# A hybrid trunk layer on one core: Hyena convolutions in two lanes that take turns, and the Hyena chunks ahead of queries, keys and values

## The chip, the cores and the metric

The kernel runs on one core of a Trainium2 chip: a matrix engine (PE, with its weight load, PEld), a vector engine (DVE), an activation engine (ACT), a general engine (POOL) and a queue engine (SP) that mostly issues DMAs. The engines run beside one another; each takes its own instructions strictly in the order of its queue. The metric is the time of one execution on the device in microseconds (us), less is better.

## The reference

One layer for 1024 latent tokens and 256 context tokens of width 1024. Half of the mixed width is attention (8 heads of 64), half a Hyena group of 512 channels with two long convolutions in a row, done by FFT:

```python
def _layer(x, mods, attend, norm1_g, w_in, hy_conv_w, hy_conv_b, k_f, filt_bias, ...):
    h = _rmsnorm(x, norm1_g) * (1.0 + sc1) + sh1
    proj = h @ w_in                                   # 1024 -> 3*512 (q, k, v) + 3*512 (hyena)
    hy = _dwconv3(proj[..., 3 * ATTN_WIDTH:], hy_conv_w, hy_conv_b)
    a = attend(q, k, v)
    hyo = _hyena(hy, k_f, filt_bias)
    merged = concat([_rmsnorm(a, ...), _rmsnorm(hyo, ...)])
    x = x + g1 * (merged @ w_out)
    h2 = _rmsnorm(x, norm2_g) * (1.0 + sc2) + sh2
    u = _dwconv3(h2 @ w_up, ffn_conv_w, ffn_conv_b)
    return x + g2 * ((silu(gate) * up) @ w_down)

def _hyena(hy, k_f, filt_bias):
    x1, x2, v = jnp.split(hy, 3, axis=-1)
    z = x1 * _long_conv(v, k_f[:, 0], filt_bias[0])
    return x2 * _long_conv(z, k_f[:, 1], filt_bias[1])
```

Latent tokens attend to an 8 x 16 neighbourhood of a 16 x 64 grid, with a learned relative bias, and to 256 cached context keys in the same softmax. The filters k_f come from a small network and an FFT of their own.

## The kernel before

The program is written once for the whole layer; a scheduler of the language then orders each engine's queue by priorities (the order of the text, which high_priority shifts ahead) and by the tiles' dependencies.

**Projection.** The product with w_in is cut into 24 chunks of 128 output channels; the first is done earlier, 23 stand in this stage. Each chunk loads its weights (tile wr, SP), splits them in two parts (wh on ACT, wl on POOL or DVE) and multiplies them in three passes with the tokens held in hh and hl (lines 116 to 118, 72 matmuls into a PSUM bank psp). A chunk of hyena channels (hy_chunk, lines 650 to 680) also does the width-3 convolution on ACT and DVE, folds the sequence (tile fo), turns it over PE and stores it in DRAM (lxd for latent, cxd for context tokens). A chunk of queries, keys or values (qkv, lines 682 to 719) goes through ACT copies to DRAM (qd, kd, vd). The loop at lines 737 to 756 takes for each j of 0 to 3 in turn one chunk of q, hyena, k, hyena, v, hyena, and after j = 0 the three tables of relative bias (rpb_frames: 16 small loads each and one store, rpw in DRAM). In between, at low density, run the filters' FFTs (psfA, psfB), which keep their data in the pool filt on the right side of the memory, and the products with w_ada.

**Chains.** When the filters are done, their pool is closed and a pool "chain" opens in its place. chain(j), lines 770 to 892, convolves 128 channels twice (o = 0, 1): a forward transform (line 802: 8 matmuls with dftf into a bank pscA, in 4 pieces; ACT makes two twisted copies t, DVE adds them, line 816), a butterfly on DVE (822 to 827), the product with the filter spectrum K loaded from DRAM (836 to 843), a butterfly back (847 to 852) with a twist (857 to 859), and an inverse transform (line 871: 8 matmuls, 2 pieces) with the gate x1 or x2. Each piece holds a bank pscA until ACT and DVE have read it. Chains 0 to 3 are latent, chain 4 (lat false) is all of the context, without the butterflies. Tiles of even and odd chains have different tags (b_ = j % 2), so that two chains may be under way, and each has one tile t (TB = 1). Each chain is written out as a whole, one after another, with a priority of 2000 places ahead. For chains 0 and 1 there are three banks pscA; then these are closed and the chains 2 to 4 have one, because attention takes seven of the eight banks.

**Attention.** Four pairs of heads (attend), each with four blocks of latent queries and the context. A block makes scores (psS, line 1038), adds the bias from a table tb (DVE, line 1059), exponentials (ACT, 1072 and 1073), turns them over PE (psX, 1082), copies them to SBUF (pt: ACT and DVE) and multiplies by values (psav, 999). POOL issues the loads of q, k, vs and of the tables (line 951, 16 per table, three tables per pair).

**Output projection.** Its pool wo_ takes the memory of the pool chain: w_out is loaded (tile wor, SP) and split (wh on ACT, line 1158, wl on DVE, line 1159) after the last chain. Then token sums (psX, line 1187), the products into psd, in two halves (attention's from tile ar, hyena's from tile mr, whose rows y are loaded from hyd, where the chains stored them), norms, then the feed-forward part, which lasts to the end.

Of the kernel before, what the change touches and what calls it, by code (L numbers as in the profile page):

```python
# [11 lines left out]
F32 = mybir.dt.float32  # L12
# [7 lines left out]
P = 128  # L20
# [3 lines left out]
LT = LL + LC  # L24
# [62 lines left out]
def _build(nc, tc, top, V, A, G, T, Q, I, O, dbg, upto):  # L87
# [412 lines left out]
    with ies:  # L500
# [3 lines left out]
        for gi, (s, col, tl) in enumerate(groups):  # L504
            xs = []
            for i in tl:
                src, row, _ = tiles[i]
# [22 lines left out]
            n = P * len(tl)  # L530
# [54 lines left out]
    ip = pool(ies, "ip", reuse_waits="tile")  # L585
# [150 lines left out]

    for j in range(4):
        for which in range(3):
            if j + which > 0:
                qkv(j, which)  # L740
            hy_chunk(which, j)
            if j + which == 0:

                t = ft([P, 512], "tm", bufs=2)
                e = "p a b -> p (a b)"
                Q.dma_start(out=t, in_=I["t_dft"].flatten().rearrange("(p x) -> p x", p=P))
                split(t, dft[0].rearrange(e), dft[1].rearrange(e))
                Q.dma_start(out=dlt, in_=I["t_delta"])
                Q.dma_start(out=nt, in_=I["t_nt"])
                with tc.issue_after(wloads[-1]):  # L750
                    Ws0 = w3load(0)
                filters(hs1, hs2, Ws0)
        cached(j)
        if j == 0:
            for var in range(3):
                rpb_frames(ip.tile([P, LT], F32, tag="fo", name="rp", bufs=1), var)
    fes.close()
    fbk.close()
    cbk = Banks("bkc", "right", "tile", cA=(1, 3))
# [8 lines left out]
    CHP = 2000  # L768

    def chain(j):  # L770

        lat = j < 4
        b_ = j % 2
# [18 lines left out]
        for o in range(2):  # L792
# [3 lines left out]
            for h in range(2):  # L796
                hs = slice(h * P, (h + 1) * P)
                for rp in range(2):
                    pa = bk("cA")
                    xs = slice(rp * 256, (rp + 1) * 256)  # L800
                    for i in range(2):
                        T.matmul(pa[:, i * 256:(i + 1) * 256], dftf[:, i, hs], uv[:, i, xs], start=True, stop=True)
                    pv = pa.rearrange("p (i r c) -> p i r c", i=2, r=2)
                    if not lat:
                        A.copy(Gv[:, h, :, 2 * rp:2 * rp + 2], pv)
                        continue
                    for ri in range(2):
                        r = 2 * rp + ri
                        if r == 0:
                            A.copy(Gv[:, h, :, 0], pv[:, :, 0])  # L810
                            continue
                        c, s, ns = tw_chain(h, r)
                        t = cp.tile([P, 2, P], F32, tag=f"t{b_}", name="t", bufs=TB)
                        A.activation(t[:, 0], pv[:, 1, ri], AF.Copy, scale=ns)
                        A.activation(t[:, 1], pv[:, 0, ri], AF.Copy, scale=s)
                        V.scalar_tensor_tensor(Gv[:, h, :, r], pv[:, :, ri], c, t, op0=ALU.mult, op1=ALU.add)
            if lat:
                ac = s4().rearrange(f4, h=2, i=2, q=2)
                X = s8()
                Xv = X.rearrange(f4, h=2, i=2, q=4)  # L820
                Xf = X.rearrange("p (h x c) -> p h x c", h=2, x=8)
                V.tensor_add(ac, Gv[:, :, :, 0:2], Gv[:, :, :, 2:4])
                V.tensor_sub(Gv[:, :, :, 2:4], Gv[:, :, :, 0:2], Gv[:, :, :, 2:4])
                V.tensor_sub(Xf[:, :, 2:8:5], Gv[:, :, :, 2], Gv[:, :, ::-1, 3])
                V.tensor_add(Xf[:, :, 3:7:3], Gv[:, :, :, 2], Gv[:, :, ::-1, 3])
                V.tensor_add(Xv[:, :, :, 0], ac[:, :, :, 0], ac[:, :, :, 1])
                V.tensor_sub(Xv[:, :, :, 1], ac[:, :, :, 0], ac[:, :, :, 1])
                Y = Gt
            else:
                X = Gt  # L830
                Y = s8()
            Xs = X.rearrange("p (h i x) -> p h i x", h=2, i=2)
            Ys = Y.rearrange("p (h i x) -> p h i x", h=2, i=2)
            for h in range(2):
                Kt = cp.tile([P, 2, 512], F32, tag=f"K{b_}", name="K", bufs=1)
                Q.dma_start(out=Kt.rearrange(f1), in_=(Kd[o, j] if lat else Kc[o])[:, h * 1024:(h + 1) * 1024])
                kr = Kt[:, 0:1].to_broadcast([P, 2, 512])
                ki = Kt[:, 1:2].to_broadcast([P, 2, 512])
                B = s4().rearrange(v2, i=2)
                V.tensor_mul(B, Xs[:, h, ::-1], ki)  # L840
                V.tensor_mul(Ys[:, h], Xs[:, h], kr)
                V.tensor_sub(Ys[:, h, 0], Ys[:, h, 0], B[:, 0])
                V.tensor_add(Ys[:, h, 1], Ys[:, h, 1], B[:, 1])
            if lat:
                ac = s4().rearrange(f4, h=2, i=2, q=2)
                Gf = Gt.rearrange("p (h x c) -> p h x c", h=2, x=8)
                V.tensor_add(ac, Gv[:, :, :, 0:4:2], Gv[:, :, :, 1:4:2])
                V.tensor_sub(Xv[:, :, :, 0:2], Gv[:, :, :, 0:4:2], Gv[:, :, :, 1:4:2])
                V.tensor_add(Gf[:, :, 1:8:6], Xv[:, :, :, 0], Xv[:, :, ::-1, 1])
                V.tensor_sub(Gf[:, :, 3:6:2], Xv[:, :, :, 0], Xv[:, :, ::-1, 1])  # L850
                V.tensor_add(Gv[:, :, :, 0], ac[:, :, :, 0], ac[:, :, :, 1])
                V.tensor_sub(Gv[:, :, :, 2], ac[:, :, :, 0], ac[:, :, :, 1])
                for h in range(2):
                    for r in (1, 2, 3):
                        c, s, ns = tw_chain(h, r)
                        t = cp.tile([P, 2, P], F32, tag=f"t{b_}", name="t", bufs=TB)
                        A.activation(t[:, 0], Gv[:, h, 1, r], AF.Copy, scale=s)
                        A.activation(t[:, 1], Gv[:, h, 0, r], AF.Copy, scale=ns)
                        V.scalar_tensor_tensor(Gv[:, h, :, r], Gv[:, h, :, r], c, t, op0=ALU.mult, op1=ALU.add)  # L859
            if o == 0:  # L860
                x1 = load(1).rearrange(v2, i=2)
                un = s4()
            else:
                x2 = load(2).rearrange(v2, i=2)
                ot = s4().rearrange(v2, i=2)
# [19 lines left out]
            if o == 0:  # L885
                u = un
            elif lat:
                for i in range(2):
                    Q.dma_start(out=hyd[i * 4:i * 4 + 4, :, j * P:(j + 1) * P].rearrange("r p c -> p r c"),
                                in_=ot[:, i].rearrange("p (r c) -> p r c", r=4))  # L890
            else:
                Q.dma_start(out=hyd[8:10].rearrange("i p x -> p i x"), in_=ot)

    for j in range(5):
        if j == 2:
            cbk.close()
            cbk = Banks("bkd", "right", "tile", cA=(1, 1))
        with tc.high_priority(offset=CHP):
            chain(j)
    for _ in ada:  # L900
        pass
    scalevec(A2, n2g, 4)
# [879 lines left out]
```

## Time and profile before

| | us |
|---|---|
| median of 3 timed runs (1921.77 to 1924.47) | 1923.5 |
| the profiled execution | 1925.38 |
| its span (first to last instruction) | 1923.4 |
| PE busy | 1742.3 (91%) |
| weight load busy | 1460.2 (76%) |
| DVE busy | 1358.3 (71%) |
| ACT busy | 893.5 (46%) |
| POOL busy | 371.1 (19%) |

Times in the rows are microseconds from the start of the span. A row of the timeline gives start, duration, engine, line, operation, the tile written and the tiles read, the count, and in brackets how long the engine had stood idle before it and what released it. The granted clock is the share of TensorE's full clock that the chip granted. A float32 matmul of the program shows as two in the trace, one with float32r operands as one. Names are those of the program; s stands for all tiles of the chains (tags s8 and s4).

### The profile page before, as it was taken

How to read it: one execution, taken by the hardware profiler on the slowest of the kernel's cores; microseconds unless marked ns; L12 is line 12 of the kernel's file. 1: busy time of each engine (PE TensorE's matmuls, PEld its weight loads, DVE VectorE, ACT ScalarE, POOL GpSimd, SP SyncE). 2: the span in 40 equal slices, each digit the busy share in tenths (PEclk: the TensorE clock that was granted, in tenths of full speed). 3: DMA queues.
4: the chain of work that ended last, by engine and by line, in shares of the span. 5: the costliest groups of instructions: out<-in, count | busy, mean ns of one | idle time of the engine just before them, and what ended most of it. 6: DMA issues, size and time to landing. Idle time of an engine off the chain costs nothing.

```text
span 1923.4 us, 27377 instructions
## 1 busy us (share of the span) xinstructions
PE 1742.3 (91%) x9999; PEld 1460.2 (76%) x9999; DVE 1358.3 (71%) x2158; ACT 893.5 (46%) x1852; POOL 371.1 (19%) x436
## 2 busy tenths in 40 slices
PE   5899989999993798866799699999999999999997
PEld 1688877888872455443688699999999999788786
DVE  4657637756776877864455888888877777666787
ACT  4654435434342677631445544444444444443352
POOL 2354545541236553200100000000000000000001
PEclk7999989999996999985799799999999999999999
DMA  7424444456445433102622155555322222844663
GB/s 261 137 75 129 130 123 123 133 166 198 132 156 151 107 71 99 48 23 66 208 99 98 55 160 165 165 164 173 113 72 72 72 66 67 295 173 124 200 196 128
DMA packets 207288, 249.75 MB, mean 130 GB/s; under 512 B 26915, under 2 KB 152980, under 8 KB 206898
## 3 DMA queue, kind: packets, MB, share of 16 engines
q1 hardware_dynamic: 196936, 231.86, 37.5%
q0 software_dynamic: 8512, 15.33, 3.2%
q8 instruction: 79, 1.29, 0.3%
q10 hardware_dynamic: 1705, 0.82, 0.2%
q14 instruction: 56, 0.45, 0.1%
HBM read 176.75 MB, written 71.20 MB: 129 GB/s over the span
## 4 chain that ended last, share of the span: by engine, by line
PE 35%; DVE 14%; DMA 8%; issue 4%; ACT 4%; POOL 2%; SPq 0%; DVEq 0%; POOLq 0%; ACTq 0%
PE psd L118 5%; PE psd L116 5%; PE psd L117 5%; DMA wt<-in_w_down_dram 2%; PE psa L116 2%; PE psa L117 2%; PE psa L118 2%; DMA tdr<-wt 2%; POOL tb L951 2%; PE psc L117 1%; PE psc L118 1%; PE psc L116 1%; PE pscA L871 1%; PE psb L117 1%; PE psb L118 1%
## 5 line engine op out<-in xcount | busy, mean ns | idle before, releaser
L116 PE MATMUL psp<-hh,wh 128*128 128x512 f32 (+1 forms) x552 | 202.3, 367 | 2.3 <-ACT wh L121 1.9
L118 PE MATMUL psp<-hh,wl 128*128 128x512 f32 (+1 forms) x552 | 200.0, 363 | 0.9 <-POOL wl L122 0.9
L117 PE MATMUL psp<-hl,wh 128*128 128x512 f32 (+1 forms) x552 | 199.1, 361 | 0.0
L116 PE MATMUL psa<-T,ws 128*128 128x256 f32 (+1 forms) x528 | 166.2, 315 | 3.1 <-ACT rows L1497 3.0
L117 PE MATMUL psa<-T,ws 128*128 128x256 f32 (+1 forms) x528 | 165.8, 314 | 2.8 <-DVE T L1224 2.8
L118 PE MATMUL psa<-T,ws 128*128 128x256 f32 (+1 forms) x528 | 165.2, 313 | 0.0
L1697 POOL TENSOR_TENSOR rs<-rs,mhalf 128x1 f32<-128x1 f32 x10 | 7.7, 772 | 813.9 <-DVE rs L1696 813.9
L116 PE MATMUL psd<-wd,gs 128*128 128x512 f32 x360 | 140.8, 392 | 3.1 <-ACT gs L121 3.1
L117 PE MATMUL psd<-wd,gs 128*128 128x512 f32 x360 | 141.0, 392 | 0.0
L118 PE MATMUL psd<-wd,gs 128*128 128x512 f32 x360 | 123.4, 390 | 2.5 <-DVE gs L122 2.5
L116 PEld LDWEIGHTS psp<-hh,wh 128*128 128x128 f32 x552 | 105.4, 191 | 23.3 <-issue 6.2
L118 PEld LDWEIGHTS psp<-hh,wl 128*128 128x128 f32 x552 | 105.5, 191 | 16.0 <-POOL wl L122 1.2
L116 PE MATMUL psc<-T,ws 128*128 128x384 f32 (+1 forms) x352 | 110.2, 313 | 7.3 <-ACT ws L121 7.3
L117 PEld LDWEIGHTS psp<-hl,wh 128*128 128x128 f32 x552 | 105.6, 191 | 14.2 <-issue 0.4
L117 PE MATMUL psc<-T,ws 128*128 128x384 f32 (+1 forms) x352 | 110.2, 313 | 0.0
L118 PE MATMUL psc<-T,ws 128*128 128x384 f32 (+1 forms) x352 | 110.0, 313 | 0.0
L117 PE MATMUL psb<-T,ws 128*128 128x384 f32 (+1 forms) x352 | 109.9, 312 | 0.0
L118 PE MATMUL psb<-T,ws 128*128 128x384 f32 (+1 forms) x352 | 109.9, 312 | 0.0
L116 PE MATMUL psb<-T,ws 128*128 128x384 f32 (+1 forms) x352 | 109.8, 312 | 0.0
L951 POOL DMA_DIRECT2D tb<-rpw x192 | 100.4, 531 | 35.7 <-DVE m L1059 20.3
L871 PE MATMUL pscA<-s,idft 128*128 128x256 f32 x160 | 55.1, 487 | 56.0 <-DVE s L859 45.1
L116 PEld LDWEIGHTS psa<-T,ws 128*128 128x128 f32 x528 | 101.4, 192 | 4.7 <-ACT rows L1497 4.7
(394 smaller groups left out, 4800.9 us busy)
## 6 DMA issues: line engine op xcount, KB each, us to landing
wada<-in_w_ada_dram SPq DMA_DIRECT2D x48, 512.0 KB
wr<-in_w_up_dram SPq DMA_DIRECT2D x44, 512.0 KB
gr<-gdr SPq DMA_DIRECT2D x44, 320.0 KB
wr<-in_w_in_dram SPq DMA_DIRECT2D x23, 512.0 KB
wt<-in_w_down_dram SPq DMA_DIRECT2D x44, 256.0 KB
tdr<-wt SPq DMA_DIRECT2D x44, 256.0 KB
gdr<-cv SPq DMA_DIRECT2D x22, 512.0 KB
wr<-tdr SPq DMA_DIRECT2D x20, 512.0 KB
```

Of the source, the lines that this page charges most:

```text
L116: T.matmul(out, ah, bh, start=start, stop=False, skip_group_check=True)
L117: T.matmul(out, ah, bl, start=False, stop=False, skip_group_check=True)
L118: T.matmul(out, al, bh, start=False, stop=stop, skip_group_check=True)
L871: T.matmul(pa[:, i * 256:(i + 1) * 256], idft[:, i, h], Ys[:, h, i, xs], start=h == 0, stop=h == 1, skip_group_check=True)
L951: G.dma_start(out=tv[:, :, a * 8:a * 8 + 64], in_=rpw[var, :, 2 * p_:2 * p_ + 2, :, d * 8:d * 8 + 64].rearrange("q h u x -> q (h u) x"))
L1697: G.tensor_tensor(rs, rs, mhalf, op=ALU.pow)
```

## The change

```diff
@@ in the input projection
     for j in range(4):
         for which in range(3):
-            if j + which > 0:
-                qkv(j, which)
             hy_chunk(which, j)
             if j + which == 0:
...
                 filters(hs1, hs2, Ws0)
+    for j in range(4):
+        for which in range(3):
+            if j + which > 0:
+                qkv(j, which)
+            if j == 0:
+                rpb_frames(ip.tile([P, LT], F32, tag="fo", name="rp", bufs=1), which)
         cached(j)
-        if j == 0:
-            for var in range(3):
-                rpb_frames(ip.tile([P, LT], F32, tag="fo", name="rp", bufs=1), var)
@@ in chain(j), four times for each o: behind the forward transform, the filter product,
@@ the butterfly back, and the inverse transform with its stores
+            yield
@@ the loop over the chains
-    for j in range(5):
-        if j == 2:
+            yield
+
+
+    lanes = [(None for j in js for _ in chain(j)) for js in ((0, 2, 4), (1, 3))]
+    turn2 = [0, 0] + [1, 0] * 20 + [0] * 8
+    for n, i in enumerate(turn2):
+        if n == 16:
             cbk.close()
             cbk = Banks("bkd", "right", "tile", cA=(1, 1))
         with tc.high_priority(offset=CHP):
-            chain(j)
+            next(lanes[i], None)
```

All twelve hyena chunks are written first, then the eleven chunks of q, k and v, with a table of relative bias behind each of the first three. chain becomes a generator of eight phases. Lane 0 runs chains 0, 2 and 4, lane 1 chains 1 and 3; after two phases of lane 0 the lanes alternate. The three banks pscA become one after 16 phases: by then chain 0 is written out, chain 1 but for its last phase, and chain 2's first forward transform. In the changed program lines 770 to 890 stand 1 to 5 lines later, and what is behind the chains 9 later (scores at 1047, the transforms at 804 and 876).

The order that the scheduler makes of it, at three places. On PE, behind the last matmul of the projection. The numbers in the names count tiles: before, s_5566 is the first convolution of chain 1, s_5660 and s_5679 its second, s_5800 the first of chain 2.

```order
L871 MATMUL pscA<-s_5566,idft 128x256
L233 MATMUL pstB<-ident,mr_4674 128x128 x2
L671 MATMUL pstB<-ident,fo 128x128 x8
L871 MATMUL pscA<-s_5566,idft 128x256 x3
L677 MATMUL pstB<-ident,fo 128x128 x2
L871 MATMUL pscA<-s_5566,idft 128x256 x3
L802 MATMUL pscA<-s_5660,dftf 128x256 x2
L732 MATMUL pstB<-ident,ck 128x128 x2
L802 MATMUL pscA<-s_5660,dftf 128x256 x6
L871 MATMUL pscA<-s_5679,idft 128x256 x8
L802 MATMUL pscA<-s_5800,dftf 128x256 x2
L1038 MATMUL psS<-k,q 128x264 x2
```

Behind the change, the same place on PE; s_5771 is the first convolution of chain 2, s_5623 the second of chain 1, s_5863 the first of chain 3.

```order
L804 MATMUL pscA<-s_5771,dftf 128x256 x6
L233 MATMUL pstB<-ident,mr_4440 128x128 x2
L704 MATMUL pstB<-ident,qkv 128x128 x2
L804 MATMUL pscA<-s_5771,dftf 128x256 x2
L716 MATMUL pstB<-ident,qkv 128x128 x8
L876 MATMUL pscA<-s_5623,idft 128x256 x4
L732 MATMUL pstB<-ident,ck 128x128 x2
L876 MATMUL pscA<-s_5623,idft 128x256 x4
L1047 MATMUL psS<-k,q 128x264 x2
L1047 MATMUL psS<-k,q 128x288 x2
L804 MATMUL pscA<-s_5863,dftf 128x256 x4
```

Before, a whole second convolution of one chain (forward, then inverse) stands between the projection and the first score; now a forward transform and an inverse one of two different chains do. Ahead of this place PE's queue before has three forward and two inverse transforms, that of the change four and three.

On PE, at the end of attention, before: s_6147 is the second convolution of chain 3, s_6264 to s_6336 both of chain 4, and the rows of line 1187 are the token sums.

```order
L999 MATMUL psav<-pt,vs 64x256 x2
L1187 MATMUL psX<-ones_71,asq 128x2
L1187 MATMUL psX<-ones_71,sq 128x2
L1187 MATMUL psX<-ones_71,asq 128x2
L1187 MATMUL psX<-ones_71,sq 128x2
L871 MATMUL pscA<-s_6147,idft 128x256 x8
L802 MATMUL pscA<-s_6264,dftf 128x256 x8
L871 MATMUL pscA<-s_6283,idft 128x256 x8
L802 MATMUL pscA<-s_6300,dftf 128x256 x8
L871 MATMUL pscA<-s_6336,idft 128x256 x8
```

And with the change, the last chain rows on PE (s_6336 is again the last convolution of chain 4), which stand in the middle of attention:

```order
L1091 MATMUL psX<-ident,Pl_6396 128x128 x2
L876 MATMUL pscA<-s_6336,idft 128x256
L1008 MATMUL psav<-pt,vs 64x256 x2
L1091 MATMUL psX<-ident,Pl_6392 128x128 x2
L1091 MATMUL psX<-ident,Pl_6396 128x128 x2
L1008 MATMUL psav<-pt,vs 64x256 x2
L1091 MATMUL psX<-ident,pc 128x128 x4
L876 MATMUL pscA<-s_6336,idft 128x256 x4
L1008 MATMUL psav<-pt,vs 64x256 x2
```

At this point 108 of the 144 score rows, 242 of the 458 rows into psX and 104 of the 192 into psav have been passed; from here to the token sums PE's queue holds attention only.

On ACT, the split of w_out (tile wh), before, between the last copies of chain 4 and the first of tile ar:

```order
L805 COPY s_6319<-pscA 128x2x256 x4
L881 COPY tt<-pscA 128x256 x2
L1158 ACTIVATE wh_8286<-wor,vec 128x1024
L1158 ACTIVATE wh_8292<-wor,vec 128x1024
L1158 ACTIVATE wh_8298<-wor,vec 128x1024
L1158 ACTIVATE wh_8304<-wor,vec 128x1024
L1251 CAST ar<-at_6387 128x512 x2
```

and with the change, where attention's copies (pt) and exponentials (pcc) stand between and behind its rows:

```order
L1000 COPY pt<-psX 128x512 x3
L1020 COPY lt<-psX 128x128
L1025 COPY bs<-psX 128x512
L1167 ACTIVATE wh_8286<-wor,vec 128x1024
L1000 COPY pt<-psX 128x512 x2
L1167 ACTIVATE wh_8292<-wor,vec 128x1024
L1000 COPY pt<-psX 128x512 x3
L1167 ACTIVATE wh_8298<-wor,vec 128x1024
L1167 ACTIVATE wh_8304<-wor,vec 128x1024
L1000 COPY pt<-psX 128x512
L1112 ACTIVATE pcc,lc<-psS,n 128x256 x4
```

The nine rows of the split moved from behind the chains to the last part of attention.

More of the change, by code (lines that the diff above doesn't have):

```diff
@@ L859, in chain @@
                         V.scalar_tensor_tensor(Gv[:, h, :, r], Gv[:, h, :, r], c, t, op0=ALU.mult, op1=ALU.add)
+            yield
             if o == 0:
@@ L892, in chain @@
                 Q.dma_start(out=hyd[8:10].rearrange("i p x -> p i x"), in_=ot)
-    for j in range(5):
-        if j == 2:
+            yield
+    lanes = [(None for j in js for _ in chain(j)) for js in ((0, 2, 4), (1, 3))]
+    turn2 = [0, 0] + [1, 0] * 20 + [0] * 8
+    for n, i in enumerate(turn2):
+        if n == 16:
             cbk.close()
```

## The prediction

> **What bounds the kernel now.** I read the busy time of each engine by stretches first, then PE's instructions in order of time at the two places where PE stands still, then the stretches of single tiles. The columns of the first view are: stretch, its length, busy time (and instructions) of PE, weight load, DVE, ACT and POOL, the granted clock, DMA share, GB/s.
>
> ```profile
> 570.00:625.00 55.00, 20.99 (x85) 13.56 (x83) 35.55 (x63) 18.67 (x57) 35.87 (x74) 0.72 0.50 141
> 625.00:848.00 223.00, 196.67 (x1256) 115.94 (x1256) 169.35 (x385) 145.59 (x472) 82.22 (x154) 0.99 0.27 71
> 848.00:937.00 89.00, 46.31 (x117) 30.98 (x117) 41.82 (x62) 16.52 (x31) 2.38 (x2) 0.56 0.26 81
> ```
>
> The reader is to see three stretches: the gap between projection and attention, the attention (PE 196.67 of 223 us, 0.88), and a tail of 89 us in which no engine reaches half its time. PE tells what stands there:
>
> ```profile
> 613.30 1.19 PE L871 MATMUL pscA<-s,idft 128*128 128x256 f32 x2 [24.70 <-DVE s L859]
> ...
> 623.42 1.20 PE L1038 MATMUL psS<-k,q 64*128 64x264 f32 x8
> ...
> 847.36 0.36 PE L1187 MATMUL psX<-ones,sq 128*128 128x2 f32 x2
> 860.23 1.22 PE L871 MATMUL pscA<-s,idft 128*128 128x256 f32 x2 [12.51 <-DVE s L859]
> ...
> 923.36 0.63 PE L1187 MATMUL psX<-ones,asq 128*128 128x2 f32 x2 [5.14 <-DVE ria L1190]
> ...
> 936.94 0.80 PE L116 MATMUL psd<-wh,ar 128*128 128x512 f32 x1 [0.77 <-ACT ar L1251]
> ```
>
> In the gap PE holds the scores (L1038) behind chain 1's second convolution and waits 24.70 us for it. In the tail it has nothing but the end of chain 3 and all of chain 4, one step behind another, and the output projection (psd) starts at 936.94. Both are **latencies of one chain at a time**, and both lie on the path.
>
> How much work the chains are shows on the tile that they live in (s; here the columns are PE, weight load, DVE, ACT, clock, DMA share, GB/s), and the last row is one whole context convolution:
>
> ```profile
> 440.00:570.00 130.00, 20.18 (x80) 14.50 (x80) 80.29 (x103) 11.69 (x34) 1.00 0.49 156
> 570.00:625.00 55.00, 17.17 (x52) 11.16 (x52) 31.98 (x50) 8.54 (x25) 0.72 0.50 141
> 625.00:848.00 223.00, 28.24 (x108) 18.71 (x108) 88.97 (x129) 15.51 (x43) 0.99 0.27 71
> 848.00:923.00 75.00, 37.65 (x80) 22.46 (x80) 36.76 (x52) 8.95 (x20) 0.57 0.21 63
> 873.00:896.00 23.00, 15.06 (x32) 8.92 (x32) 10.85 (x15) 2.34 (x4) 0.55 0.30 92
> ```
>
> The DVE column of the first four rows adds up to 238 us, for ten convolutions: 2 x 10.85 for the context, so (238 - 22)/8 = 27 us for each of the eight latent ones. On PE a transform of 16 such matmuls (8 in the program, two passes each) costs 28.24/108 x 16 = 4.2 us in the attention.
>
> **The change part by part.** Nothing is computed more or less. What moves is counted from the order above, and each term is a point in time of the profiled execution.
>
> *End of the projection.* The last projection matmul releases POOL here:
>
> ```profile
> 570.39 0.20 POOL L968 MEMSET Pl<- 128x120 f32 x1 [4.27 <-PE psp L118]
> 572.31 7.37 POOL L951 DMA_DIRECT2D tb<-rpw  x14
> ```
>
> so it ended at 570.4. The order of before has five transforms ahead of that point (three forward, two inverse, less the last matmuls), that of the change seven (four and three). PE is full there (second row below), so two more transforms add 2 x 4.2 = 8.4: **579**. What could shift this is the earlier stall in the first row:
>
> ```profile
> 250.00:300.00 50.00, 40.59 (x207) 32.39 (x207) 26.98 (x44) 23.20 (x53) 27.59 (x20) 0.83 0.41 129
> 440.00:570.00 130.00, 129.03 (x721) 105.27 (x721) 97.72 (x148) 50.64 (x119) 29.07 (x17) 1.00 0.49 156
> ...
> 262.78 10.10 SPq L556 DMA_DIRECT2D rp<-in_rpb_dram  x13
> ...
> 275.03 0.39 SPq L606 DMA_DIRECT2D wr<-in_w_in_dram  x1
> ```
>
> PE loses 9.4 us there, and SP's queue issues 13 bias loads for 10.10 us ahead of the next chunk's weights. The same 48 loads now stand between chunks 16 and 19, ahead of other weight loads: the stall may go (-9), stay, or come twice (+9). I take it as staying. That all hyena chunks run beside the filters puts about 12 x 4 us of convolution on DVE into the first half instead of half of it; PE's cover there is the reason to cost it at nothing, and the +9 holds what it costs if the cover fails.
>
> *First score.* PE's queue now has one forward transform of chain 2 and chain 1's last inverse ahead of the first score, both of which have been prepared by different lanes. DVE's queue, however, has chain work ahead of the first score row: the end of chain 1 and chain 2 up to its filter product, some 25 us of the 27 above. Without any idle that is 25 us; in the gap of before one lane needed 42 us (from 580 to 622) for about as much. Two lanes fill each other's waits, but not all: 33, so **612** instead of 623. The first bias table is ready long before (14 of its 16 loads are issued by 579.7 in POOL's row above, 9 us behind the projection). POOL's queue now has 4 loads of the next pair ahead of the second table, which wait for the first scores; 4 + 16 loads at 0.53 us (7.37/14) are 11 us, and DVE has some 30 us of rows before the second table is read, so they stay hidden.
>
> *Attention with chains.* At the last inverse transform PE's queue of the change has passed 108 of 144 score rows, 242 of 458 rows into psX and 104 of 192 into psav; what follows is attention alone. From the first score to there DVE has 27 x 4 of chains (6 of chain 2's first convolution, then three whole ones and the two of the context: 6 + 81 + 22 = 109 us) and its own work: 169.35 - 88.97 = 80 us in all, of which between 53% and 75% by those counts; scores weigh more on DVE, so 55. Together **165 us**. PE's own work is 196.67 - 28.24 = 168 us, divided like these rows (columns as for s):
>
> ```profile
> 625.00:848.00 223.00, 48.04 (x280) 23.99 (x280) 52.53 (x83) 43.89 (x160) 0.99 0.27 71
> 625.00:848.00 223.00, 78.10 (x484) 53.10 (x484) 21.87 (x32) 45.54 (x88) 0.99 0.27 71
> 625.00:848.00 223.00, 59.23 (x384) 20.79 (x384) 7.15 (x12) 0.99 0.27 71
> ```
>
> (psS, psX, psav). A quarter of the first, 43% of the second (without the 36 rows of the token sums) and 46% of the third remain: 72 of 185, so 66 of the 168. The first part has 102 + 11 transforms x 4.2 = 149 us for PE. DVE has more and is the bound. In the attention of before the busier engine had 0.88 of the time: 165/0.88 = 188, **800**. The bounds: 165 with no idle at all, 217 if DVE stays at the 169.35/223 = 0.76 that it had. What idles it there is the chain's own handshake with ACT, 23.3 us in 24 steps:
>
> ```profile
> L816 DVE SCALAR_TENSOR_TENSOR s<-pscA,tw,t 128x256 f32<-128x256 f32 x24 | 11.5, 481 | 23.3 <-ACT t L815 23.3
> ```
>
> In the new order rows of the other lane or of scores stand between most of these steps, so I go above 0.76.
>
> *Attention alone.* 66/0.88 = 75: **875**. PE reached more where the chains were quiet:
>
> ```profile
> 810.00:847.00 37.00, 35.97 (x227) 22.05 (x228) 22.02 (x38) 20.35 (x59) 0.00 (x0) 0.95 0.01 1
> ```
>
> (0.97, hence 68 as the lower bound). I stay at 0.88 because w_out's split now stands here, nine ACT copies of about 1.1 us and as many DVE rows, and the first waits for a load, 8.39 us in ACT's row of before:
>
> ```profile
> 927.06 2.19 ACT L1158 ACTIVATE wh<-wor,vec 128x1024 fp32r<-128x1024 f32 x2 [8.39 <-DMA wor<-in_w_out_dram]
> ```
>
> With that wait laid open the term is 85 (75 + 8, and 2 for later loads).
>
> *Start of the output projection.* From the first token sum behind the chains to the first psd matmul the rows above show 923.36 to 936.94, 13.6 us at half clock and with the weights still to load. At full clock and with weights ready: 9 (bounds 7 and 14), **884**. What is late next are the hyena rows y, which load only when attention's memory is free; two tokens' attention half of the product (48 matmuls) covers them as before. From psd on nothing changes.
>
> Sum: 936.94 - 884 = 53 us less. The profiled execution took 1925.38 (its span 1923.4), 1.9 over the median of 1923.5; the same 53 from the median give **1871**.
>
> A place where the notes speak against the change. The row first: the 108 matmuls of the chains took 28.24 us at clock 0.99, the 80 of the tail 37.65 at 0.57, 1.8 times as much each. The Trainium skill, TensorE: Matmul & The Clock Gate, section "What's actually happening", says that PE drops to half clock after an idle window of about 3.4 us and needs as long a busy one to return. The trace agrees in the tail. By the rule a first part that DVE bounds, with PE 149/188 busy, could fall to half clock as well; it is a rival below.
>
> **The rivals.**
>
> *DVE stays at 0.76* (217 instead of 188, and the wait for w_out is exposed, +10): 1871 + 39 = 1910. For it: each lane keeps a single t buffer. Against: the interleaved order. 0.14.
>
> *The lanes fill everything*: 25, 165 and 68 in place of 33, 188 and 75: 1871 - 38 = 1833. For it: tens of us in which DVE was full. Against: DVE's queue is in order. 0.10.
>
> *Slower: one PSUM bank for two lanes.* From the change of banks on, both lanes take turns in one bank, through all of the first part. How long it is held shows in chain 2 of before:
>
> ```profile
> 677.55 1.46 PE L871 MATMUL pscA<-s,idft 128*128 128x256 f32 x6
> 680.96 1.99 PE L871 MATMUL pscA<-s,idft 128*128 128x256 f32 x8
> 685.96 1.03 PE L802 MATMUL pscA<-s,dftf 128*128 128x256 f32 x4
> 690.30 1.13 PE L802 MATMUL pscA<-s,dftf 128*128 128x256 f32 x4
> ```
>
> 4.3 us for a forward and 3.4 for an inverse piece; 20 and 12 of them are 127 us, hidden in 188. If DVE's longer queue stretches each hold, the bank decides from 188/127 = 1.5 times on, and the gain is gone at (188 + 53)/127 = 1.9 times; at twice, 254, it is 1871 + 66 = 1937. 0.04.
>
> *Slower: the clock.* All 149 us of PE's first part at the tail's price are 1.8 x 149 = 268 instead of 188: 1951. Break-even is at three quarters of it. Against it:
>
> ```profile
> 640.00:650.00 10.00, 7.20 (x45) 3.70 (x44) 10.00 (x24) 5.39 (x19) 4.99 (x10) 1.00 0.23 39
> ```
>
> PE at 0.72 with DVE full, and the clock is 1.00. 0.03. This is what the rule of the Trainium skill would do here.
>
> *The wait only moves*: attention ends as early, but something else holds psd until about 937, the final time 1923. The rows of the new order between the last score and psd hold no chain and no weight split, so 0.02.
>
> **How the numbers follow.** Forecast 0.67, the rest as given. 0.2% of the time is 3.8 us, about what a measurement of this kernel can tell from no change. Faster by more: 0.67 + 0.14 + 0.10, less 0.01: 0.90; within: 0.03; slower: 0.07. All lower bounds together give 570 + 25 + 165 + 68 + 7 = 835, so 1822; all upper ones 588 + 42 + 217 + 85 + 14 = 946, so 1932; they don't all fall one way. The range takes in the first rival and half of the second: 1840 to 1910.
>
> **What would show it.** The last projection matmul near 579, the first score near 612, no chain row behind the last score, DVE at 0.85 or more and the clock at 1.0 until the last inverse transform near 800, psd from 884 at full clock, and the same 986 us from there to the end. I am wrong if DVE idles on ACT's t as often as before, if attention's copies wait for w_out in ACT's queue, if PE waits for chains before 579, or if the first product of the output projection waits for y.

## The result, and the profile after

The changed kernel takes **1870.95 us** (median of 4 runs, 1868.46 to 1874.61) against 1922.63 us for the one before (4 runs beside them, 1915.45 to 1924.47): ratio 0.9739, 95% interval 0.971 to 0.9769, so 52 us by the medians and 2.6% by the ratio, where 1871 us had been predicted. Its profiled execution took 1868.46 us, with a span of 1866.7.

The total fits to a microsecond, the way there does not. First the stretches of the changed kernel that answer to those of before (stretch, length, busy us of PE, weight load, DVE, ACT and POOL, granted clock, DMA share, GB/s):

```profile
250.00:300.00 50.00, 49.12 (x317) 41.20 (x316) 31.10 (x57) 28.10 (x57) 24.58 (x17) 1.00 0.39 125
567.00:591.00 24.00, 13.91 (x49) 10.78 (x48) 17.23 (x32) 11.67 (x41) 15.62 (x37) 0.72 0.57 151
591.00:793.00 202.00, 159.92 (x865) 95.89 (x863) 167.59 (x348) 112.26 (x362) 96.74 (x181) 0.87 0.41 115
793.00:868.00 75.00, 67.49 (x465) 38.65 (x464) 39.18 (x88) 49.15 (x131) 5.55 (x11) 1.00 0.23 70
868.00:880.00 12.00, 8.87 (x43) 8.64 (x42) 1.25 (x6) 2.78 (x4) 2.38 (x2) 0.62 0.07 24
```

The tail of 89 us with one chain alone is gone: behind the last inverse transform stand 75 us of attention alone, in which PE works 0.90 of the time, and 12 us of token sums. The gap has shrunk from 53 us (570.39 to 623.42) to 24. Row one holds a surprise: PE is nearly full between 250 and 300 us (49.12 of 50 us), where it lost 9.4 us before. Row three holds the other one: the attention with chains takes 202 us, and the clock in it is 0.87.

The points themselves, from the changed kernel's instructions in order of time (start, us, engine, line; in brackets how long the engine stood idle before, and for what):

```profile
567.54 0.20 POOL L977 MEMSET Pl<- 128x120 f32 x1 [9.45 <-PE psp L118]
...
591.53 1.20 PE L1047 MATMUL psS<-k,q 64*128 64x264 f32 x8
...
602.68 2.04 PE L804 MATMUL pscA<-s,dftf 128*128 128x256 f32 x4 [9.95 <-DMA s<-lxd]
...
791.19 1.89 PE L876 MATMUL pscA<-s,idft 128*128 128x256 f32 x8
...
867.92 0.28 PE L1196 MATMUL psX<-ones,asq 128*128 128x2 f32 x2
...
880.73 0.77 PE L116 MATMUL psd<-wh,ar 128*128 128x512 f32 x1
```

| point | before | predicted | measured | the step: predicted, measured |
|---|---|---|---|---|
| last projection matmul | 570.4 | 579 | 567.5 | +8.6, -2.9 |
| first score | 623.4 | 612 | 591.5 | gap 33, 24 |
| end of the last inverse transform | | 800 | 793.1 | attention with chains 188, 201.6 |
| end of attention (first token sum) | 846.7 | 875 | 867.9 | attention alone 75, 74.8 |
| first psd | 936.9 | 884 | 880.7 | 9, 12.8 |
| end of the span | 1923.4 | | 1866.7 | 986.5 before, 986.0 |

Up to psd 56.2 us are saved instead of 53; the errors of the five steps are -11.5, -9, +13.6, -0.2 and +3.8 us and mostly cancel. That the time was met to a microsecond is luck. The experiments ask which of the steps were understood.

### The profile page after: what moved, and what is told of

Same layout as the page of the kernel before. It is cut to its first block, busy times and chain, and to the rows that moved or that the text cites. A ratio compares the mean times of both kernels' runs of the same rounds, so it can differ in the third digit from the quotient of the medians.

```text
span 1866.7 us, 27362 instructions
## 1 busy us (share of the span) xinstructions
PE 1728.6 (93%) x9999; PEld 1453.5 (78%) x9999; DVE 1365.0 (73%) x2158; ACT 891.3 (48%) x1852; POOL 366.3 (20%) x436
## 4 chain that ended last, share of the span: by engine, by line
PE 50%; DVE 22%; DMA 12%; issue 6%; ACT 6%; POOL 2%; SPq 1%; DVEq 0%; ACTq 0%; POOLq 0%
PE psd L116 6%; PE psd L117 6%; PE psd L118 6%; PE psp L116 2%; PE psp L118 2%; PE psp L117 2%; PE psa L116 2%; PE psa L117 2%; PE psa L118 2%; DMA wt<-in_w_down_dram 2%; DMA tdr<-wt 2%; PE psc L117 2%; PE psc L118 2%; PE psc L116 2%; PE psav L1008 1%
## 5 line engine op out<-in xcount | busy, mean ns | idle before, releaser
L116 PE MATMUL psp<-hh,wh 128*128 128x512 f32 (+1 forms) x552 | 201.6, 365 | 1.9 <-ACT wh L121 1.9
L116 PEld LDWEIGHTS psa<-T,ws 128*128 128x128 f32 x528 | 101.1, 192 | 7.4 <-ACT rows L1506 7.4
L117 PEld LDWEIGHTS psa<-T,ws 128*128 128x128 f32 x528 | 101.2, 192 | 3.1 <-DVE T L1233 3.1
```

Of the source, the lines that this page charges most:

```text
L116: T.matmul(out, ah, bh, start=start, stop=False, skip_group_check=True)
L117: T.matmul(out, ah, bl, start=False, stop=False, skip_group_check=True)
```

## The experiments

Each ratio is against the kernel before, run beside the experiment on the same chip; there its median was 1920.0 to 1922.7 us, so medians of different experiments compare only to some 3 us. The points come from each one's profiled execution, in us; "attention" is first score to its end.

| run | last projection matmul | first score | end of attention | first psd | attention | median us | ratio, 95% interval |
|---|---|---|---|---|---|---|---|
| before | 570.4 | 623.4 | 846.7 | 936.9 | 223 | 1922.63 | 1 |
| the change | 567.5 | 591.5 | 867.9 | 880.7 | 276 | 1870.95 | 0.9739 (0.971 to 0.9769) |
| e1_order | 559.8 | 624.9 | 853.4 | 937.0 | 229 | 1932.23 | 1.0048 (1.0031 to 1.0065) |
| e2_lanes | 584.9 | 614.3 | 882.3 | 895.1 | 268 | 1874.84 | 0.9763 (0.9742 to 0.9785) |
| e3_ctx_last | 571.7 | 596.3 | 877.8 | 890.6 | 282 | 1874.07 | 0.9744 (0.972 to 0.9769) |
| e5_before_rpb | 568.9 | 633.9 | 860.6 | 946.3 | 227 | 1936.77 | 1.0083 (1.0068 to 1.0098) |
| e6_rpb_end | 567.1 | 594.5 | 871.8 | 884.6 | 277 | 1865.15 | 0.9719 (0.9692 to 0.9747) |
| e7_qkv_later | 570.0 | 590.4 | 864.9 | 877.9 | 274 | 1863.48 | 0.9702 (0.9684 to 0.9721) |
| e8_t3 | 568.9 | 587.8 | 871.4 | 884.4 | 284 | 1872.12 | 0.9751 (0.9735 to 0.9766) |
| e9_all | 571.6 | 586.1 | 858.4 | 871.2 | 272 | 1858.81 | 0.9686 (0.966 to 0.9712) |
| e10_end_later | 565.3 | 593.3 | 870.8 | 883.8 | 277 | 1871.23 | 0.9745 (0.9729 to 0.9761) |
| e11_bank8 | 565.4 | 587.5 | 866.0 | 878.8 | 278 | 1863.47 | 0.9702 (0.9685 to 0.9719) |
| e12_dve_more | 563.2 | 603.6 | 852.9 | 868.9 | 249 | 1858.84 | 0.9678 (0.9663 to 0.9694) |
| e13_spread | 570.7 | 599.5 | 857.7 | 872.3 | 258 | 1854.03 | 0.9642 (0.96 to 0.9683) |

### Which half of the change does it

**e1_order**: the projection in the new order, the chains one after another.

```diff
+    for j in range(5):
+        if j == 2:
+            cbk.close()
+            cbk = Banks("bkd", "right", "tile", cA=(1, 1))
+        with tc.high_priority(offset=CHP):
+            for _ in chain(j):
+                pass
-    lanes = [(None for j in js for _ in chain(j)) for js in ((0, 2, 4), (1, 3))]
...
```

> The projection in the new order (hyena chunks first, bias frames in three portions), the chains one after another as before. Theory (the lanes bring the gain, the order only removes the stall between 250 and 300 us): PE's queue is that of before behind the projection, so gap and tail stay (first score some 40 us or more behind the last projection matmul, a tail of 89 us), and only the 9 to 12 us of the stall go: 1913 us, between 1908 and 1918. Rival (the chains' inputs come earlier by the order, and that is much of the gain): 1900 or less.

**e2_lanes**: the lanes, with the projection loop of before (each chunk's `qkv` ahead of its `hy_chunk`, all bias frames behind the first group).

> The two lanes with the projection in the old order. Theory: the gap and the tail shrink as in the full change and the stall between 250 and 300 us comes back with its 9 to 12 us: 1880 us, between 1876 and 1886. Rival (the lanes need the hyena chunks early): the last chunk's projection ends late, chain 3 starts late, and the lanes lose half of their gain: 1895 or more.

The lanes alone give 0.9763, nearly all of the gain; the order alone gives none, and is even 0.5% slower. The trace of e1 says why there is no gain:

```profile
559.78 0.20 POOL L976 MEMSET Pl<- 128x120 f32 x1 [4.88 <-PE psp L118]
...
614.36 1.19 PE L876 MATMUL pscA<-s,idft 128*128 128x256 f32 x2 [25.77 <-DVE s L863]
...
624.85 1.20 PE L1046 MATMUL psS<-k,q 64*128 64x264 f32 x8
...
937.01 0.79 PE L116 MATMUL psd<-wh,ar 128*128 128x512 f32 x1 [0.54 <-ACT ar L1259]
```

The projection ends 10.6 us earlier, as the theory had it, but the first score stands where it stood (624.85 against 623.42), and psd too (937.01 against 936.94): ahead of the first score PE waits 25.77 us for a step of the one chain (24.70 before), so an earlier end of the projection only makes the gap longer. This half of the theory for e1 (9 to 12 us gained) was wrong. That its median is some 10 us above before is not seen in this trace, whose own execution took 1925.94 us; where these 10 us lie stays open.

The time of e2 is 1 us below the range of its theory (1876 to 1886). Its projection ends 17.4 us later than the change's: the stall is back (PE 40.68 of the 50 us from 250 on), and its trace has eight transforms ahead of the last projection matmul in place of seven. Its psd comes 14.4 us later, but in an execution of 1882.23 us; the medians are only 4 us apart and the intervals overlap. By the ends of the two intervals the order adds to the lanes anything from 5 us lost to 14 gained, so its gain is not shown.

### Where the stall of the projection went

**e5_before_rpb**: the kernel before, with the bias frames behind the third group of chunks.

```diff
         cached(j)
-        if j == 0:
+        if j == 2:
             for var in range(3):
                 rpb_frames(...)
```

> The kernel before, with nothing changed but that the three bias frames with their 48 loads are made behind the third group of chunks in place of the first. Theory S1 (SP's queue, full of bias loads, held back the loads for which PE waited between 250 and 300 us): the stall goes, PE is busy 48 or more of these 50 us, and 9 to 12 us are gained: 1913 us. Rival S2 (the stall comes from the order in which hyena chunks, queries, keys and values alternate beside the filters): PE stays near 41 of 50 us and the time near 1923 us.

Two stretches of e5:

```profile
250.00:300.00 50.00, 50.00 (x312) 42.33 (x313) 26.53 (x43) 24.05 (x52) 22.94 (x14) 1.00 0.47 148
...
500.00:550.00 50.00, 35.72 (x169) 26.89 (x168) 34.76 (x47) 15.29 (x39) 15.42 (x10) 0.80 0.40 122
```

The stall leaves its place with the 48 loads, as S1 says, and comes back at theirs with 14.3 us instead of 9.4. POOL's queue in e5 shows the way it takes, and PE's last row what waits for it:

```profile
506.92 0.58 POOL L557 COPY rp<-rp 128x480 f32<-128x480 f32 x1 [13.02 <-DMA rp<-in_rpb_dram]
508.19 2.34 POOL L122 TENSOR_TENSOR wl<-wr,wh 128x1024 fp32r<-128x1024 f32 x1 [0.69 <-ACT wh L121]
512.21 2.40 POOL L663 TENSOR_TENSOR fo<-cv 128x512 f32<-128x512 f32 x1 [1.68 <-DMA rpw<-rp]
514.66 1.12 PE L671 MATMUL pstB<-ident,fo 128*128 128x128 f32 x4 [7.55 <-POOL fo L663]
```

POOL's copy of a frame waits 13 us for its 16 loads, and behind it in the same queue stand the split of the next weights (`wl`) and the next hyena chunk's sums (`fo`, which use the frames' buffer: one tag, one buffer). PE waits 7.55 us for that `fo`. The first score comes 10.5 us later than before (633.9), and the kernel is slower by 0.8%, where S1 had promised 9 to 12 us of gain. In before a neighbouring effect is seen: a filter's weights (`csl`) stood in SP's queue behind bias loads, and POOL waited for them with everything behind it:

```profile
238.63 7.82 SPq L556 DMA_DIRECT2D rp<-in_rpb_dram  x11
246.55 0.53 SPq L353 DMA_DIRECT2D csl<-in_filt_w_dram  x1
...
251.42 1.71 POOL L360 TENSOR_TENSOR cs<-csl 128x512 f32<-128x512 f32 x1 [13.12 <-DMA csl<-in_filt_w_dram]
```

PE's wait for these weights is 2.53 of its 9.4 us. Most of the rest falls between 270 and 295 us, where the filters' steps have no projection matmul beside them from 275 on; e5 shows that this goes too when the loads go, but not by which path.

With all hyena chunks first, the frames come when no hyena chunk is left behind them and the filters are nearly through: at 365 to 435 us in the changed kernel, where PE loses 5.5 us of 50 (400 to 450).

**e6_rpb_end** moves the frames further, behind the loads of `dftf` and `idft`, so that the chains can begin earlier.

```diff
-            if j == 0:
-                rpb_frames(..., which)
...
     Q.dma_start(out=idft...)
+    for var in range(3):
+        rpb_frames(..., var)
```

> The full change, with the three bias frames made behind the loads of the chains' own matrices (dftf, idft) in place of beside the first queries, keys and values. In PE's order the first transform stands 22 projection matmuls (about 8 us) earlier. Theory (the chains' start sets the first score, as the run with the order alone suggests): the first transform starts near 441 instead of 448.8, the first score comes 5 to 8 us earlier, 1862 to 1866 us. Rival (the projection's end and what DVE has to do behind it set the first score): first score near 591 again, 1868 to 1873 us.

The first transform starts at 444.11 instead of 448.76, but the first score at 594.5 and not earlier. The median, 1865.15 us, lies in the theory's range, but the ratio cannot be told from the change's, and the profiled execution (1872.46) lies in the rival's. The theory that the chain's start sets the first score isn't borne out for two lanes; nor for one chain in e1, where the first transform starts 8.7 us later than before (448.8 against 440.1) and the first score only 1.4.

### What the order of the lanes can bear

**e3_ctx_last**: the context chain alone behind the other four.

```diff
-    lanes = [... for js in ((0, 2, 4), (1, 3))]
+    lanes = [... for js in ((0, 2), (1, 3), (4,))]
-    turn2 = [0, 0] + [1, 0] * 20 + [0] * 8
+    turn2 = [0, 0] + [1, 0] * 14 + [1] * 2 + [2] * 8
```

> The full change, but the context chain (4) is taken alone behind the other four, as one lane. Theory (the tail went because the chains end while attention is left to run beside them): the last inverse transform comes later and about 8 to 13 us less of attention stand behind it, PE still has attention to fill, and the time is 1868 to 1878 us. Rival (a chain alone costs its latency again): two convolutions of 23 us come back, 1905 to 1915 us.

0.9744: no loss that these runs can tell from the change. The last inverse transform ends at 809 instead of 793 and attention covers it. The 46 us that chain 4 cost in before were no price of being alone, but of having nothing left beside it.

**e11_bank8** changes one number: the lanes share the single PSUM bank after 8 phases.

```diff
-        if n == 16:
+        if n == 8:
```

> The full change with the move of the chains into the single PSUM bank after 8 phases in place of 16. Theory (one bank is held 127 us of 202 and is no bound): within 6 us of the full change, 1865 to 1877 us. Rival (the single bank makes the lanes wait for each other): half of the 40 latent and context phases fall back toward one chain at a time, the first score or the last inverse transform comes 15 us or more later, 1882 us or more.

0.9702, 1863.47 us: 1.5 us below the theory's range, with an interval that overlaps the change's. It is not slower, and the rival of the single bank falls.

### What makes the attention with chains slow

**e7_qkv_later**. In the changed kernel POOL issues the next pair's q, k and vs from 591.58 on (2 MB), and SP 1.3 us later the load that chain 3 begins with (start, us, engine, line):

```profile
591.58 0.56 POOL L965 DMA_DIRECT2D q<-qd  x1 [8.41 <-issue]
...
592.90 0.32 SPq L790 DMA_DIRECT2D s<-lxd  x1
```

In its chain of work that ended last (start, us, what) this load has 9.64 us:

```profile
592.90 9.64 DMA s<-lxd
```

PE stands behind it for 9.95 us (the row at 602.68 above). The edit holds the pair's loads behind its first bias table:

```diff
-        q, k = qkload(p_) if p_ else first
-        vs = tp.tile(...)
-        G.dma_start(out=vs...)
+        last = bias_load(p_, 0) if p_ else None
+        with tc.issue_after(last) if p_ == 1 else ExitStack():
+            q, k = qkload(p_) if p_ else first
+            vs = tp.tile(...)
+            G.dma_start(out=vs...)
...
```

> The full change, with the next pair's loads of q, k and vs held behind the first new bias table, so that they are not on the DMA engines when chain 3's first input is loaded (592.90 us, 9.64 us to land). Theory (these 2 MB slow the load, and PE stands behind it): the load lands within 6.5 us, PE's wait of 9.95 us is at most 6, and the first part ends 4 to 6 us earlier, 1863 to 1867 us. Rival (the load is slow for other reasons, or DVE has too much else to do for it to matter): within 2 us of the full change, 1868 to 1873 us.

The trace of e7, first the load, then the matmul that waits for it, then where the pair's loads are now:

```profile
593.37 0.32 SPq L790 DMA_DIRECT2D s<-lxd  x1
...
597.17 2.05 PE L804 MATMUL pscA<-s,dftf 128*128 128x256 f32 x4 [5.58 <-DMA s<-lxd]
...
629.35 0.57 POOL L966 DMA_DIRECT2D q<-qd  x1
```

PE starts 3.8 us after the load's issue instead of 9.8, with the same 512 KB: beside the 2 MB of another queue it had taken longer. The Trainium skill, DMA: Bandwidth & Descriptors, section "Issuing engines are not separate DMA queues", says that transfers interleave on the same 16 engines whichever engine starts them; the trace agrees. PE's wait is 5.58 us, and the time lies in the theory's range: 7.5 us lower by the medians, 4.9 when each is taken against its own kernel before, and the two intervals just overlap. In the profiled execution psd comes 2.9 us earlier, and the attention is only 1.9 us shorter.

**e8_t3**: the t tiles of both lanes in one pool of three (the same line at both places where t is made).

```diff
-  t = cp.tile([P, 2, P], F32, tag=f"t{b_}", name="t", bufs=TB)
+  t = cp.tile([P, 2, P], F32, tag="t", name="t", bufs=3)
```

> The full change, with one pool of three t buffers for both lanes in place of one buffer for each lane. In PE's order the last inverse transform now stands behind 124 of the 144 score rows in place of 108. Theory (the single t buffers make DVE wait for ACT, 15.4 us in 9 waits at L818): these waits fall below 8 us and the end of attention comes 5 to 10 us earlier, 1859 to 1865 us. Rival (ACT's own queue makes the wait, the copies come late whatever their buffers): the waits stay near 15 us, 1868 to 1873 us.

No gain, and the wait of DVE for t at the forward twiddle is 19.5 us instead of 15.4. A third buffer does not shorten it.

**e9_all** (e6, e7 and e8 together) and **e10_end_later** (e6 and e7):

> The full change with the three edits together: bias frames behind the chains' matrices, the next pair's loads held back, three shared t buffers. If the three limits are apart from each other the gains add up: 1848 to 1858 us. If one engine bounds the first part whatever is removed (DVE, 0.83 busy there) they don't: 1860 to 1870 us.

> The full change with two of the three edits: bias frames behind the chains' matrices, and the next pair's loads held back; one t buffer for each lane as in the change. If the third t buffer is worth nothing (it alone gave 1872 us), this is as fast as the three together or faster: 1856 to 1861 us. If the buffer pays once the load is out of the way, this is slower than the three together: 1862 to 1866 us.

Each against its own kernel before, and compared with the change, e6, e7 and e8 gave -3.2, -4.9 and +3.8 us, e9 -9.5 and e10 +2.3. So e9 gains more than its three edits do apart, and e10 gives nothing (0.9745). The time of e9 lies between its two ranges, that of e10 above both of its own. Single edits do not simply add up here; each also makes the scheduler write another order of all rows, which may be why. Why e9 gains and e10 does not stays open.

**e12_dve_more** puts more work on the engine that the prediction called the bound:

```diff
             B = s4().rearrange(v2, i=2)
-            V.tensor_mul(B, Xs[:, h, ::-1], ki)
-            V.tensor_mul(Ys[:, h], Xs[:, h], kr)
+            for _ in range(2):
+                V.tensor_mul(B, Xs[:, h, ::-1], ki)
+                V.tensor_mul(Ys[:, h], Xs[:, h], kr)
```

> The full change with the two multiplications of each filter product done twice (2.44 us more on DVE for each half of a convolution: about 15 us beside the projection, 2 in the gap, 27 in the attention with chains). Theory (DVE bounds the attention with chains and the gap): most of the 27 + 2 us come out, attention ends 20 to 29 us later, 1888 to 1899 us. Rival (DVE's idle share there, 0.17 of 202 us, or attention's last part without chains takes it up): 1871 to 1879 us.

Neither: it is **faster** than the change by 12 us (10 when each is taken against its own kernel before), with all that work added. The attention of the change, and then that of e12, from first score to end:

```profile
591.50:867.90 276.40, 226.81 (x1325) 134.25 (x1325) 206.27 (x435) 161.41 (x493) 102.29 (x191) 0.91 0.36 103
```

```profile
603.60:852.90 249.30, 218.35 (x1333) 130.42 (x1333) 225.38 (x459) 152.34 (x486) 85.13 (x160) 0.97 0.33 89
```

With 19 us more on DVE it is 27 us shorter (of which 12 pay for the later first score): DVE at 0.90 instead of 0.75, and the clock at 0.97. So the amount of work on DVE was not what bounded the 276 us. What differs is the order. The scheduler, given longer steps of the chains, has spread them: counted in PE's order by sixteenths of the score rows, the change has 28 transform matmuls in the first three and none behind the thirteenth; e12 has 12 in the first three and goes on to the end. The early and the late attention of the change:

```profile
591.00:620.00 29.00, 14.22 (x44) 8.40 (x43) 18.01 (x36) 11.65 (x41) 13.88 (x25) 0.62 0.61 187
620.00:650.00 30.00, 18.57 (x81) 10.87 (x79) 27.53 (x47) 8.48 (x25) 14.58 (x29) 0.73 0.34 86
...
793.00:830.00 37.00, 33.52 (x229) 19.06 (x228) 23.37 (x47) 24.75 (x60) 5.55 (x11) 1.00 0.44 134
830.00:868.00 38.00, 33.97 (x237) 19.59 (x237) 15.81 (x42) 24.40 (x72) 0.00 (x0) 1.00 0.03 8
```

From 620 to 650 DVE is nearly full (27.53 us, 24.16 of them chains), PE works 18.57 of 30 us and its clock is 0.73; from 830 on DVE has less than half to do. In its first 60 us the attention of e12 has about as much chain work on DVE as the change (40.79 us on tile s, the doubled rows included, against 39.52), but PE gets 32 us of attention done beside it instead of 16. In e12 PE's wait for chain 3's load, 13.19 us, falls ahead of the first score.

**e13_spread** does the same on purpose, without the extra work:

```diff
+    phases(17, CHP)
...
+    PLAN = iter([2, 2, 2, 2, 2, 2, 2, 2, 2, 2, 2, 1])
...
             m2 = stat("n", 4)
-            V.tensor_reduce(m2, ...)
+            red = V.tensor_reduce(m2, ...)
...
             Pc[cb] = pc
+            phases(next(PLAN, 50), CHP, red.ins)
```

(`phases(n, offset, after)` takes the next n turns of the lanes, each queued behind the instruction `after` on its engine. The three banks become one after 17 phases instead of 16.)

> The full change with the same work, but from the 17th phase on two phases are queued behind each score block of the attention (an order on DVE's queue), so that the chains reach over all 16 blocks in place of 12, with no more than 12 transform matmuls in any one of them (16 in the second block before). Theory (the attention with chains is slow because the chains crowd its first blocks, not because DVE has too much work; that is why more DVE work, which spread the chains, was faster): from the first score to the end of attention 245 to 255 us in place of 275, 1842 to 1855 us. Rival (the gain of the run with doubled multiplications has another source): 268 us or more, 1863 to 1876 us.

1854.03 us, the lowest median of all; its interval (0.96 to 0.9683) lies wholly below the change's, but overlaps those of e9 and e12. Its attention:

```profile
599.50:857.70 258.20, 221.90 (x1323) 132.50 (x1322) 206.15 (x437) 157.05 (x489) 99.15 (x186) 0.92 0.36 101
```

DVE does 206.15 us as in the change (206.27), in 258 us instead of 276; that is 3 us more than the theory had expected, and 10 below the rival's 268. The first score comes 8 us later, so 10 of the 18 us are left at the end of attention. Order alone, on the same work, moved this. In the first 60 us DVE has 38.77 us of chains, as in the change, but PE does 30 us of attention beside them instead of 16.

That the spreading itself is the cause isn't shown apart, because two things moved with it. Chain 3's first transform, whose wait for its load is 9.95 us of the change's attention, stands ahead of the first score here (5.00 us); and that load is issued ahead of the next pair's loads, not behind them:

```profile
593.35 0.37 SPq L790 DMA_DIRECT2D s<-lxd  x1
...
595.36 0.56 POOL L969 DMA_DIRECT2D q<-qd  x1 [7.97 <-issue]
...
597.48 2.04 PE L804 MATMUL pscA<-s,dftf 128*128 128x256 f32 x4 [5.00 <-DMA s<-lxd]
```

From the last projection matmul to the end of attention e13 takes 286.9 us, the change 300.4, e12 289.7; but e9 takes 286.8, and its trace has 22 transform matmuls in the first three sixteenths (e13 has 10).

## Why the prediction was right, and where its steps were not

**The mechanism held.** Gap and tail were the latency of one chain at a time (e1 without the lanes keeps both), the lanes take most of it away (e2 has them without the new order), and attention covers what is left (e3). The 986 us behind psd did not move. The rival that the wait only moves is out.

**End of the projection, 579 against 567.5.** The two more transforms are there: e1, with five of them ahead, ends its projection at 559.8, the change with seven at 567.5, 7.7 us for two where 8.4 were predicted. The term that failed is the stall between 250 and 300 us, which I took as staying. The diff moved its cause, and the row quoted for it (13 bias loads, 10.10 us in SP's queue) pointed at it; e5 shows that the stall goes with those loads. "The stall may go" was the right case, the choice was not.

**First score, 612 against 591.5.** The gap was taken as 33 us between bounds of 25 (no idle) and 42 (one lane); it came out at 24. DVE's work there was less than the 25 us counted: 17.23 us in the gap. The rest was done earlier, as tile s shows (stretch, length, PE, weight load, DVE, ACT, clock, DMA share, GB/s):

```profile
440.00:567.00 127.00, 27.76 (x112) 20.36 (x112) 97.84 (x136) 15.71 (x44) 1.00 0.53 164
567.00:591.50 24.50, 12.33 (x32) 8.97 (x32) 17.45 (x30) 4.91 (x14) 0.72 0.57 151
591.50:794.00 202.50, 54.39 (x177) 34.97 (x176) 113.62 (x167) 23.68 (x62) 0.87 0.41 115
```

In 127 us beside the projection the two lanes have 97.84 us of chains done on DVE; in before it was 80.29 in 130. The sum reckoned with the order of the rows and not with what two lanes get done while PE is still projecting.

**Attention with chains, 188 against 201.6.** The DVE work was well counted, 167.59 us against 165; PE's 149 became 160. The factor 0.88 was the weak term, measured 0.83, and so was its reason. "DVE has more and is the bound" is refuted as far as the amount of DVE's work goes: e12 added work to DVE and the attention became shorter. Most of the loss lies in its first 60 us, where PE stands idle for 26 of the 50 us that it idles in all of the attention, at a granted clock of 0.67. The wait for chain 3's load is 9.95 us of it, and most of the other waits there are for steps on DVE. In e12 and e13 PE idles 15 and 19 us in these 60, and both end attention earlier; but in e11 it is 17, and the attention is no shorter (278 us, with 24 more of the chains' matmuls in it). How much is due to the crowding and how much to the load is therefore not settled. A third t buffer (e8) does not help.

**The clock rival came true in part.** In the last row above 54.39/177 is 307 ns for each of the chains' matmuls, between the 261 of before's attention and the 471 of its tail. 46 ns on 177 matmuls are 8 us of PE time, an estimate, and PE's whole busy time in the stretch is 11 us above the sum's 149; both are nearer to the forecast than to the rival's 80.

**Attention alone** came out as predicted, 75 us; the wait for w_out was not laid open.

**Start of the output projection, 9 against 12.8.** I had counted on full clock; it fell to 0.50 in the token sums, as told below.

So the mechanism was right and the size of the gain about right, though only one of five terms was exact; an earlier end of the projection and a gap that closed better than expected paid for an attention that was slower. The range (1840 to 1910) had been made for such errors, and every version of the lanes that was run lies inside it.

## What to carry to other kernels

When a chain of small dependent steps stands at the end of a kernel, take it in lanes, and look at where in the covering work it then lies: in an order that spread it over all of the attention the kernel was 17 us faster by the medians than with it packed at the front, with the same instructions. An engine that is busy for 0.83 of a stretch is not shown to be its bound; add work to it and see, and look at what else the added work moved. Bulk loads that are not yet needed are worth holding back when a chain's small load has to land, and loads moved off one in-order queue's critical place must be looked for at their new place, because the wait may go with them.

## What the hardware did that was not expected

The token sums fell to a granted clock of 0.50 right behind an attention at 1.00, and stayed there while PE was busy. Fine stretches of the changed kernel:

```profile
868.00:869.00 1.00, 0.87 (x9) 0.78 (x8) 0.26 (x1) 0.58 (x1) 0.00 (x0) 1.00 0.00 0
869.00:870.00 1.00, 0.45 (x2) 0.45 (x2) 0.49 (x2) 0.54 (x1) 0.37 (x1) 1.00 0.00 0
870.00:872.00 2.00, 1.52 (x8) 1.47 (x8) 0.32 (x2) 0.52 (x1) 0.36 (x1) 0.71 0.03 8
872.00:876.00 4.00, 4.00 (x18) 4.00 (x19) 0.00 (x0) 0.00 (x0) 0.00 (x0) 0.50 0.00 0
...
884.00:890.00 6.00, 6.00 (x27) 4.81 (x26) 0.00 (x0) 0.98 (x1) 0.00 (x0) 0.96 1.03 405
```

PE's idle between 868 and 872 is about 1.2 us in all. Then it issues matmuls of two columns without a break (0.61 us a pair instead of 0.36) and the clock stays at 0.50; it comes back about 4 us into the 512-column matmuls of psd, which begin at 880.73. The Trainium skill, TensorE: Matmul & The Clock Gate, section "What's actually happening", has the drop after an idle window of about 3.4 us and the return after as long a busy one; the return fits psd, the drop and the missing return here do not, if a two-column matmul counts as busy. Whether it doesn't was not tried.
